# A hybrid encoder layer: half of two sets of transposes moved from the DMA queue to TensorE, a third buffer for the weights of down, and another order at the end of gate/up

## The chip, the cores and the metric

One NeuronCore of a Trainium2 chip runs the whole kernel. The metric is the device time of one execution in microseconds; the profile is one further execution, recorded instruction by instruction. Engines are TensorE (PE), VectorE (DVE), ScalarE (ACT), GpSimd (POOL) and SyncE (SP), which here issues all DMAs, in order.

## The reference

One layer over 2048 rows of width 1024, in f32:

```python
h = rmsnorm(r, norm1_g)
proj = h @ w_in                                   # q k v z beta alpha lx lg
dn_out  = rmsnorm(deltanet(fwd) + deltanet(bwd)) * silu(z)   # 4 heads, chunks of 64
lru_out = rmsnorm(gelu(lg) * (rglru(fwd) + rglru(bwd)))
r = r + concat([dn_out, lru_out]) @ w_out
h2 = rmsnorm(r, norm2_g)
gate = dwconv(h2 @ ffn_wg, ffn_conv_w) + ffn_conv_b
r = r + (gelu(gate) * (h2 @ ffn_wu)) @ ffn_wd     # width 2816
pg = sigmoid(rmsnorm(r, ple_norm_g) @ ple_wg + ple_bg)
return rmsnorm(r + pg * (p @ ple_wp), final_g)
```

## The kernel before, in words

Every large product is made from f16 halves: a number is split into a high part (ACT, a copy to f16) and the low rest (DVE, a subtraction), and three products hi x hi, lo x hi, hi x lo add up in PSUM. Gate/up and down use Strassen's scheme besides: seven products of half-size blocks, whose operands are sums of blocks that POOL adds before the split (`operands`, L1648; `split`, L1635). All of SBUF is one tile, `arena`, from which buffers are taken while the program is built.

**The order.** Each piece of work is a Python generator that yields `st(engine=price)` ahead of an instruction, `W(event)` to wait for another piece, `M(sizes)` for memory. `Sched.run` (L244) is a list planner: with the listed prices in ns it keeps a clock for each engine and always emits next the step that can start first, plus a small handicap for its priority (`LOOK` 20 ns for each step of priority). `ahead(ns)` is a DMA whose issuer does not wait. What it emits is the program; each engine and SP run their instructions in that order. A price thus changes no work, only the order. Prices that stand here: a DMA transpose 1300 (`norm`), 700 (`norm_pairs`, `ple`), 1000 (`out_lru`); the scan of the RG-LRU `c_tt(2048)`, some 2200 (L901).

**Start.** `norm1` (L653) loads x in blocks of four tiles of 128 rows; `norm` (L619) squares them (ACT, L632), forms the inverse root (`rsqrt`, eleven small DVE steps, L358 to L378), and for each tile splits the scaled row into h (ACT, L639) and l (DVE, L641) in one of three 4 KB buffers and transposes both by one DMA (L643) into `xT[b]`, the moving operand. `main` (L2485) runs the first three projections (q1, k1, lx1) quarter by quarter, one quarter for each block, and the small beta/alpha product (L787) with them; then the other projections follow. Weights go through `wprep` (L513): load, gain (POOL, L541), squares (ACT, L560), a sum over partitions (PE, L570), a power-of-two scale, split (L595, L597). `setup` (L459) forms constants on the side.

**Mixer.** Heads are prepared (`prep_head`), then run in a serial chain of 16 chunks, both directions together, one head after the other (`chain_head`, L1357); the RG-LRU streams run beside them.

**Output and normed rows.** `out_dn` (L1606), then `out_lru` (L1573) multiply the 16 tiles with w_out in the order `TILES`, and `out_add` (L1547) adds to the residual. As soon as two tiles are done, `norm_pairs` (L1717) squares them (L1736), forms the inverse root, scales them into `hb` (ACT, L1743), writes the residual out (L1747) and forms the seven right operands of Strassen's scheme from the four blocks of 128 x 512: sums on POOL, split (L1640, L1642) into one of four 2 KB buffers, and a DMA transpose (L1760) into `hU[u]`. There are eight pairs; `hU[0]` takes the first four, `hU[1]` the rest. Gate/up's unit (0, 0) needs `hU[0]`, unit (0, 1) `hU[1]`, and the first product of (0, 1) comes after four of (0, 0) (`units`, L1694).

**Gate/up, the seam, down.** `ffn` (L1998) runs 22 x 2 units (PE L1690), each evacuated by ACT (L1882) and DVE (L1887); convolution and gelu, POOL's multiplication (L1950), and a split of the result to DRAM (`act_post`, L1955). With the units of n = 20 done, `down_weights` (L2090) starts in two streams with one 8 KB raw buffer each: blocks 0, 2, 4, ... and 1, 3, 5, ... of w_d are loaded (L2100), combined on POOL (L1669) and split (L1644, L1646). Beside it run the products of p (`p_products`, L2332) and the first unit of down (`down_first`, L2202; PE L2233), which takes the blocks in order as they are ready. Then down runs seven more units, and the gated embedding follows (`ple`, L2397).

Of the kernel before, what the change touches and what calls it, by code (L numbers as in the profile page):

```python
# [16 lines left out]
S = SEQ = 2048  # L17
# [12 lines left out]
NI = 3  # L30

# [120 lines left out]
class Sched:  # L152
# [91 lines left out]
    def run(self):  # L244
        while self.streams:
# [37 lines left out]
LOOK = 20  # L283
PER = 2
# [56 lines left out]
class Kern:  # L341
# [117 lines left out]
    def setup(self):  # L459
# [32 lines left out]

        keep = self.keep
# [125 lines left out]
    def norm(self, rows, dst, done, hl, waits=()):  # L619
# [15 lines left out]
        def one(i):  # L635
            j, buf = yield from hl.take()
            h, l = buf.f16(D), buf.f16(D, at=2 * KB)
            yield st(act=c_act(D, 1))
            nc.scalar.activation(h, rows[i], AF.Copy, scale=y[:, i : i + 1])  # L639
            yield st(dve=c_stt(D))  # L640
            nc.vector.scalar_tensor_tensor(l, rows[i], y[:, i : i + 1], h, op0=ALU.mult, op1=ALU.subtract)  # L641
            yield st(dma=1300)
            nc.sync.dma_start_transpose(dst[i], buf.f16(2 * D))  # L643
            hl.done(j)
# [5 lines left out]
        for i in range(n):  # L650
            S.spawn(one(i), 3)

    def norm1(self, b, xb, hl):  # L653
# [17 lines left out]
        for o in range(0, 4, n):  # L671
            if b == 1 and o:
                yield W("xT", 0)
            ids = range(o, o + n)
            dst = [Tv[:, :, i * 128 : i * 128 + 128] for i in ids]
            S.spawn(self.norm([xb[4 * b + i].f32(D) for i in ids], dst, lambda i, o=o: done(o + i), hl, [W("x", 4 * b + i) for i in ids]), 1 if b else 0)
# [173 lines left out]
    def lru(self, ct):  # L850
# [26 lines left out]
        for d in range(2):  # L877
# [23 lines left out]
            yield st(dve=c_tt(SEQ))  # L901
# [455 lines left out]
    def chain_head(self, h):  # L1357
# [4 lines left out]
        if h:  # L1362
            yield W("chained", h - 1)
# [104 lines left out]
    def dn_out(self, h):  # L1468
# [9 lines left out]
        groups = ([6, 7, 8, 9], [4, 5, 10, 11], [2, 3, 12, 13]) + (([0, 1, 14, 15],) if h < 3 else ([1, 14], [0, 15]))  # L1478
# [94 lines left out]
    def out_lru(self):  # L1573
# [5 lines left out]
        def fetcher():  # L1579
            for j, t in enumerate(TILES):  # L1580
# [3 lines left out]
                yield ahead(1000)  # L1584
# [132 lines left out]
    def norm_pairs(self):  # L1717
# [8 lines left out]
        def begin(i):  # L1726
# [12 lines left out]
            if i == 7:  # L1739
                S.fire("last pair")  # L1740
            for k, t in enumerate(ts):
                yield st(act=c_act(D, 1))
                nc.scalar.activation(hb.f32(2, D)[:, k], self.rt(t), AF.Copy, scale=y[:, k : k + 1])  # L1743
# [10 lines left out]
            v = [hb.f32(2, D)[:, k, z * 512 : z * 512 + 512] for z in range(2) for k in range(2)]  # L1754
# [242 lines left out]

    def ffn(self):  # L1998
        S, A = self.S, self.A
        self.blk = yield M(8 * KB, 8 * KB)  # L2000
# [23 lines left out]
        def begin(n, u):  # L2024
            def f():
                if u == 0:
# [693 lines left out]
```

## Time and profile before

| | us |
|---|---|
| median of 3 runs (2795.54 to 2804.08) | 2795.77 |
| the profiled execution | 2800.17 |
| its span, first to last instruction | 2798.5 |
| PE busy (91%) | 2554.9 |
| DVE busy (65%) | 1827.6 |
| ACT busy (53%) | 1479.7 |
| POOL busy (33%) | 925.8 |

Mean granted clock of PE: 0.967 of full speed. In the lines of the profile, `L441` is the line of the kernel that made an instruction; a helper's line stands for all that call it. `arena<-arena` with a DMA is a transfer inside SBUF, here a transpose. `<-` in brackets names what ended the idle time before.

### The profile page before, as it was taken

How to read it: one execution, taken by the hardware profiler on the slowest of the kernel's cores; microseconds unless marked ns; L12 is line 12 of the kernel's file. 1: busy time of each engine (PE TensorE's matmuls, PEld its weight loads, DVE VectorE, ACT ScalarE, POOL GpSimd, SP SyncE). 2: the span in 40 equal slices, each digit the busy share in tenths (PEclk: the TensorE clock that was granted, in tenths of full speed). 3: DMA queues.
4: the chain of work that ended last, by engine and by line, in shares of the span. 5: the costliest groups of instructions: out<-in, count | busy, mean ns of one | idle time of the engine just before them, and what ended most of it. 6: DMA issues, size and time to landing. Idle time of an engine off the chain costs nothing.

```text
span 2798.5 us, 40157 instructions
## 1 busy us (share of the span) xinstructions
PE 2554.9 (91%) x13944; PEld 1291.9 (46%) x13944; DVE 1827.6 (65%) x3845; ACT 1479.7 (53%) x3094; POOL 925.8 (33%) x662
## 2 busy tenths in 40 slices
PE   5998899888989997995998999999997799999998
PEld 2554454466556664442443444444443244444443
DVE  6668877768785677486656777767768832222468
ACT  6576766764666675265655666666656410101323
POOL 1134434626320000033446566666655500000000
PEclk9999999999999998997999999999999999999999
DMA  9332242375455468488123333333326754457963
GB/s 243 80 91 80 60 133 61 88 224 167 107 160 166 124 205 290 121 194 189 58 81 100 98 104 103 102 104 104 103 64 200 232 174 144 165 166 236 278 170 139
DMA packets 479660, 399.21 MB, mean 143 GB/s; under 512 B 204897, under 2 KB 408673, under 8 KB 479457
## 3 DMA queue, kind: packets, MB, share of 16 engines
q1 hardware_dynamic: 479456, 396.64, 48.6%
q8 instruction: 110, 1.80, 0.3%
q14 instruction: 94, 0.76, 0.1%
HBM read 229.82 MB, written 128.97 MB: 128 GB/s over the span
## 4 chain that ended last, share of the span: by engine, by line
PE 50%; DVE 7%; ACT 3%; DMA 3%; issue 2%; POOL 2%; SPq 0%; ACTq 0%; DVEq 0%; POOLq 0%
PE P L1690 35%; PE P L441 12%; DVE arena L1646 2%; POOL arena L1669 1%; DMA arena<-arena 1%; PE P L2233 1%; ACT arena L1644 1%; DVE arena L1936 1%; DVE arena L1934 1%; DMA arena<-actd 1%; PE P L1427 1%; DVE arena L1642 0%; ACT arena L1640 0%; ACT arena L1736 0%; DMA arena<-in_w_gu_dram 0%
## 5 line engine op out<-in xcount | busy, mean ns | idle before, releaser
L1690 PE MATMUL P<-arena 128*128 128x512 f16 x5166 | 1132.9, 382 | 55.6 <-ACT arena L1882 30.9
L441 PE MATMUL P<-arena 128*128 128x512 f16 x4224 | 998.2, 386 | 34.9 <-DMA arena<-arena 11.9
L1690 PEld LDWEIGHTS <-arena 128*128 128x128 f16 x5166 | 508.3, 99 | 670.3 <-issue 55.3
L441 PEld LDWEIGHTS <-arena 128*128 128x128 f16 x4224 | 414.6, 100 | 483.8 <-issue 51.3
L1646 DVE SCALAR_TENSOR_TENSOR arena<-arena 128x512 f16<-128x512 f32 (+2 forms) x408 | 418.3, 1059 | 139.2 <-ACT arena L1644 138.8
L1644 ACT ACTIVATE arena<-arena 128x512 f16<-128x512 f32 (+2 forms) x408 | 281.2, 723 | 304.3 <-POOL arena L1669 144.8
L1669 POOL TENSOR_TENSOR arena<-arena 128x512 f32<-128x512 f32 (+1 forms) x200 | 343.2, 1722 | 276.0 <-DVE arena L1646 176.7
L2135 DVE SCALAR_TENSOR_TENSOR arena<-P,arena 128x512 f32<-128x512 f32 x95 | 70.0, 749 | 224.7 <-PE P L1690 189.7
L1806 POOL TENSOR_TENSOR arena<-arena 128x1024 f32<-128x1024 f32 x44 | 107.3, 2455 | 319.3 <-DMA arena<-in_w_gu_dram 310.1
L1950 POOL TENSOR_TENSOR arena<-arena 128x512 f32<-128x512 f32 x88 | 138.0, 1588 | 79.9 <-ACT arena L1940 47.9
L1882 ACT ACTIVATE arena<-P 128x512 f32<-128x512 f32 x176 | 102.5, 587 | 89.8 <-PE P L1690 73.1
L1225 POOL TENSOR_TENSOR arena<-arena 128x512 f32<-128x512 f32 x64 | 119.0, 1875 | 80.3 <-DVE arena L1175 62.7
L702 DVE SCALAR_TENSOR_TENSOR arena<-P,arena 128x511 f32<-128x511 f32 (+1 forms) x192 | 141.6, 741 | 2.0
L2186 ACT ACTIVATE arena<-arena 128x1024 bf16<-128x1024 f32 x16 | 16.9, 1056 | 236.0 <-DVE arena L2135 227.0
L1887 DVE TENSOR_TENSOR arena<-P,arena 128x512 f32<-128x512 f32 x132 | 90.0, 683 | 36.6 <-PE P L1690 35.7
L541 POOL TENSOR_TENSOR arena<-arena 128x1024 f32<-128x1024 f32 (+1 forms) x25 | 51.4, 2060 | 173.0 <-DMA arena<-in_w_in_dram 173.0
L1422 ACT ACTIVATE arena<-P,arena 128x128 f32<-128x128 f32 x128 | 46.8, 365 | 84.7 <-PE P L1416 59.9
L1433 DVE SCALAR_TENSOR_TENSOR arena<-arena,P 128x128 f32<-128x128 f32 x128 | 43.7, 342 | 52.7 <-PE P L1428 23.9
L1427 PE MATMUL P<-arena 128*128 128x128 f32 x256 | 60.4, 319 | 19.3 <-ACT arena L1425 12.7
L1547 DVE SCALAR_TENSOR_TENSOR arena<-P,arena 128x512 f32<-128x512 f32 x64 | 47.7, 746 | 43.2 <-PE P L441 43.2
L865 PE MATMUL P<-arena 128*128 128x512 f32 x128 | 64.8, 621 | 11.8 <-DVE arena L702 5.2
L1128 POOL TENSOR_TENSOR arena<-arena 128x512 f32<-128x512 f32 x32 | 39.2, 1226 | 109.4 <-DVE arena L1125 90.8
(233 smaller groups left out, 3384.8 us busy)
## 6 DMA issues: line engine op xcount, KB each, us to landing
arena<-hd SPq DMA_DIRECT2D x160, 256.0 KB, 3.2
actd<-arena SPq DMA_DIRECT2D x148, 256.0 KB, 2.4
arena<-actd SPq DMA_DIRECT2D x49, 640.0 KB, 4.0
arena<-in_w_gu_dram SPq DMA_DIRECT2D x44, 512.0 KB, 4.4
arena<-in_x_dram SPq DMA_DIRECT2D x32, 512.0 KB, 6.3
at<-arena SPq DMA_DIRECT2D x64, 256.0 KB, 2.8
arena<-at SPq DMA_DIRECT2D x128, 128.0 KB, 3.1
rd<-arena SPq DMA_DIRECT2D x32, 512.0 KB, 3.1
```

Source lines behind the costliest of these rows:

```text
L441: self.nc.tensor.matmul(out, l, r, start=(i + j == 0), stop=(i + j == m - 1))
L702: nc.vector.scalar_tensor_tensor(a[:, lo:hi], P[:, lo - sh : hi - sh], tp[:, j : j + 1], a[:, lo:hi], op0=ALU.mult, op1=ALU.add)
L1225: nc.gpsimd.tensor_tensor(pv[:, i % 2], a(slice(2 * i, 2 * i + 2)), b(slice(2 * i, 2 * i + 2)), op=ALU.mult)
L1427: nc.tensor.matmul(slot[0], k, tv[:, 2], start=True, stop=True)
L1644: nc.scalar.activation(hi, x, AF.Copy, scale=scale)
L1646: nc.vector.scalar_tensor_tensor(lo, x, scale, hi, op0=ALU.mult, op1=ALU.subtract)
L1669: nc.gpsimd.tensor_tensor(v[at], v[p], v[q], op=ALU.add if plus else ALU.subtract)
L1690: self.nc.tensor.matmul(out, l, r, start=(p in (1, 2, 5) and i + j == 0), stop=(p in (2, 3, 4) and i + j == m - 1), skip_group_check=True)
L1806: nc.gpsimd.tensor_tensor(v[i], v[i], c["g2"][:, :, None].to_broadcast([128, KT, 128]), op=ALU.mult)
L1882: nc.scalar.activation(d, P, AF.Copy)
L1887: nc.vector.tensor_tensor(d, P, d, op=ALU.add)
L1950: nc.gpsimd.tensor_tensor(v, v, U.buf.f32(2, 2, 4, 128)[:, i, s], op=ALU.mult)
```

## The change

**Start.** For blocks 0 and 1 of x (`TURN = 2`) `norm` scales the row in f32 (DVE), transposes it in eight pieces of 128 x 128 on PE into two PSUM banks (`turned`), copies the high part from PSUM (ACT) and subtracts (DVE, from PSUM), both straight into `xT`. Blocks 2 and 3 are left as they were. Priorities change (0 for turned tiles, 4 for the norms of blocks 1 to 3); the second half of block 1 no longer waits for block 0, and `setup`'s constants now do.

**Normed rows.** Pairs 1, 3, 5 and 7 transpose the four scaled blocks on PE, ACT copies them back over `hb`, and the seven operands are formed from the transposed blocks and split straight into `hU`. Pairs 0, 2, 4 and 6 are left.

**Prices.** DMA transposes: 2600 for 1300, 1400 for 700 and for 1000; the scan twice. From the units of n = 20 to the end of down's first unit (`more`) every nonzero price is raised, by 75 on ACT and by 250 on DVE and POOL.

**w_d.** Three streams with a raw buffer each: blocks (0, 3, 6, 8, 10), (1, 4, 7, 9), (2, 5).

`HEADS` is (0, 1, 2, 3), the order that stood there.

```diff
@@ Sched.run
             for e, c in cost.items():
                 if e in self.t:
+                    c += OVER[e] if c else 0
                     self.t[e] = t + c
+OVER = dict(pe=0, act=0, dve=0, pool=0, dma=0)
+SEAM = dict(act=75, dve=250, pool=250)
@@ setup
+        yield W("xT", 0)
         keep = self.keep
@@ norm
+    def turned(self, x, b):
+        P = self.bank(b)
+        for i in range(0, 512, 128):
+            self.nc.tensor.transpose(P[:, i : i + 128], x[:, i : i + 128], self.c["ident"])
+        return P
...
+            if turn:
+                yield W("ones")
+                v = buf.f32(D)
+                yield st(dve=c_tt(D) / 2)
+                nc.vector.tensor_scalar(v, rows[i], y[:, i : i + 1], None, op0=ALU.mult)
+                for k in (0, 4):
+                    b = yield st(pe=4 * 160, bank=1)
+                    P = self.turned(v[:, 128 * k : 128 * k + 512], b).rearrange("p (a n) -> p a n", n=128)
+                    yield st(act=c_act(512))
+                    nc.scalar.activation(dst[i][:, k : k + 4], P, AF.Copy)
+                    yield st(dve=c_tt(512))
+                    nc.vector.tensor_tensor(dst[i][:, 8 + k : 12 + k], P, dst[i][:, k : k + 4], op=ALU.subtract)
+                    S.release(b)
+                hl.done(j)
...
-            yield st(dma=1300)
+                yield st(dma=2600)
...
-            S.spawn(one(i), 3)
+            S.spawn(one(i), 0 if turn else 3)
@@ norm1
-            if b == 1 and o:
-                yield W("xT", 0)
...
-            S.spawn(self.norm(...), 1 if b else 0)
+            S.spawn(self.norm(..., b < TURN), 4 if b else 0)
@@ lru
-            yield st(dve=c_tt(SEQ))
+            yield st(dve=2 * c_tt(SEQ))
             nc.vector.tensor_tensor_scan(...)
@@ out_lru
-                yield ahead(1000)
+                yield ahead(1400)
@@ norm_pairs
+            if i % 2:
+                for x in v:
+                    b = yield st(pe=4 * 160, bank=1)
+                    P = self.turned(x, b)
+                    yield st(act=c_act(512))
+                    nc.scalar.activation(x, P, AF.Copy)
+                    S.release(b)
             def put(n, x):
+                if i % 2:
+                    to = self.hU[u][n].f16(8, 512)[:, :, o : o + 128]
+                    yield from self.split(x.rearrange("p (a n) -> p a n", n=128), to[:, 0:4], to[:, 4:8], 512)
+                    return
...
-                yield st(dma=700)
+                yield st(dma=1400)
@@ ffn
+    def more(self, n):
+        OVER.update(((e, n * c) for e, c in SEAM.items()))
     def ffn(self):
+        self.more(0)
...
+                if n == 20:
+                    self.more(1)
@@ down_weights
-        js = ((0, 2, 4, 6, 8, 10), (1, 3, 5, 7, 9))[par]
+        js = RAWS[par]
...
-            yield st(dma=2900, lag=0 if j == par else 3000)
+            yield st(dma=2900, lag=0 if j == js[0] else 3000)
@@ down
         yield from self.down_first(self.down_unit(0), bufs)
+        self.more(0)
@@ ple
-                    yield st(dma=700)
+                    yield st(dma=1400)
@@ main
-        for i in range(2):
+        for i in range(3):
             S.spawn(self.down_weights(i), 2)
```

More of the change, by code (lines that the diff above doesn't have):

```diff
@@ L30 @@
 NI = 3
+TURN = 2
+RAWS = ((0, 3, 6, 8, 10), (1, 4, 7, 9), (2, 5))
+HEADS = (0, 1, 2, 3)
 TILES = (7, 8, 6, 9, 5, 10, 4, 11, 3, 12, 2, 13, 1, 14, 0, 15)
@@ L616, in ring_stream, with norm @@
         self.S.fire("ring", par)
-    def norm(self, rows, dst, done, hl, waits=()):
+    def turned(self, x, b):
[3 more added lines that the diff above has]
+        return P
+    def norm(self, rows, dst, done, hl, waits=(), turn=False):
         nc, A, S = self.nc, self.A, self.S
@@ L636, in one @@
             j, buf = yield from hl.take()
[L637 to L641, printed above, removed]
-            yield st(dma=1300)
-            nc.sync.dma_start_transpose(dst[i], buf.f16(2 * D))
-            hl.done(j)
+            if turn:
[12 more added lines that the diff above has]
+                hl.done(j)
+            else:
+                h, l = buf.f16(D), buf.f16(D, at=2 * KB)
+                yield st(act=c_act(D, 1))
+                nc.scalar.activation(h, rows[i], AF.Copy, scale=y[:, i : i + 1])
+                yield st(dve=c_stt(D))
+                nc.vector.scalar_tensor_tensor(l, rows[i], y[:, i : i + 1], h, op0=ALU.mult, op1=ALU.subtract)
+                yield st(dma=2600)
+                nc.sync.dma_start_transpose(dst[i], buf.f16(2 * D))
+                hl.done(j)
             left[0] -= 1
@@ L671, in norm1 @@
         for o in range(0, 4, n):
-            if b == 1 and o:
-                yield W("xT", 0)
             ids = range(o, o + n)
             dst = [Tv[:, :, i * 128 : i * 128 + 128] for i in ids]
-            S.spawn(self.norm([xb[4 * b + i].f32(D) for i in ids], dst, lambda i, o=o: done(o + i), hl, [W("x", 4 * b + i) for i in ids]), 1 if b else 0)
+            S.spawn(self.norm([xb[4 * b + i].f32(D) for i in ids], dst, lambda i, o=o: done(o + i), hl, [W("x", 4 * b + i) for i in ids], b < TURN), 4 if b else 0)
             for i in ids:
@@ L1740, in begin @@
                 S.fire("last pair")
+            hv = hb.f32(2, D)
             for k, t in enumerate(ts):
                 yield st(act=c_act(D, 1))
-                nc.scalar.activation(hb.f32(2, D)[:, k], self.rt(t), AF.Copy, scale=y[:, k : k + 1])
+                nc.scalar.activation(hv[:, k], self.rt(t), AF.Copy, scale=y[:, k : k + 1])
             smb.free()
@@ L1753, in begin @@
             yield W("hT", u)
-            v = [hb.f32(2, D)[:, k, z * 512 : z * 512 + 512] for z in range(2) for k in range(2)]
+            v = [hv[:, k, z * 512 : z * 512 + 512] for z in range(2) for k in range(2)]
+            if i % 2:
[5 more added lines that the diff above has]
+                    S.release(b)
             def put(n, x):
+                if i % 2:
+                    to = self.hU[u][n].f16(8, 512)[:, :, o : o + 128]
+                    yield from self.split(x.rearrange("p (a n) -> p a n", n=128), to[:, 0:4], to[:, 4:8], 512)
+                    return
                 j, buf = yield from ring.take()
                 yield from self.split(x, buf.f16(512), buf.f16(512, at=KB), 512)
-                yield st(dma=700)
+                yield st(dma=1400)
                 nc.sync.dma_start_transpose(self.hU[u][n].f16(8, 512)[:, :, o : o + 128], buf.f16(1024))
@@ L2528, in main @@
                     end(G, then)
-        for h in range(4):
+        for h in HEADS:
             S.spawn(self.prep_head(h), PR["prep"])
```

11 lines of the change are left out of this document (6 added, 5 removed).

## The prediction

> **What bounds the kernel now.** The page's first line gives the span; the profiled execution took 2800.2 us, 1.7 us of it outside the span. It lies 4.4 us above the median of the three runs (2795.8), so I sum against 2800.2 and take the sum off 2795.8.
>
> ```profile
> span 2798.5 us, 40157 instructions
> ```
>
> Then the table of stretches, cut where TensorE (PE) changes its work. Columns: stretch, length, busy time and instructions of PE, weight loads, DVE, ACT, POOL; then clock, DMA share, GB/s.
>
> ```profile
> 0.00:31.00 31.00, 1.76 (x6) 1.50 (x6) 19.99 (x74) 18.42 (x28) 5.57 (x12) 1.00 0.80 210
> 31.00:56.00 25.00, 20.64 (x174) 10.36 (x175) 17.03 (x62) 18.32 (x28) 5.69 (x3) 0.97 1.07 284
> 56.00:100.00 44.00, 44.00 (x365) 22.48 (x364) 27.28 (x62) 15.62 (x22) 0.00 (x0) 0.94 0.65 138
> 100.00:210.00 110.00, 105.72 (x573) 57.59 (x572) 75.22 (x182) 83.57 (x152) 37.04 (x33) 1.00 0.29 84
> 210.00:840.00 630.00, 554.94 (x4048) 323.82 (x4046) 495.76 (x1142) 403.34 (x1070) 279.09 (x277) 0.95 0.42 120
> 840.00:1081.00 241.00, 218.72 (x1433) 150.90 (x1432) 160.98 (x595) 172.64 (x495) 11.19 (x5) 0.96 0.59 186
> ...
> 1171.00:1258.00 87.00, 86.41 (x389) 38.79 (x390) 65.59 (x146) 48.83 (x82) 28.84 (x21) 0.96 0.85 184
> 1258.00:1302.00 44.00, 12.63 (x47) 4.86 (x44) 31.44 (x70) 26.46 (x45) 19.04 (x15) 0.67 1.03 235
> ...
> 1400.00:1540.00 140.00, 123.72 (x553) 55.44 (x552) 85.26 (x109) 76.06 (x126) 76.78 (x43) 0.94 0.29 89
> ...
> 2100.00:2241.00 141.00, 102.88 (x435) 43.49 (x432) 118.10 (x130) 76.53 (x116) 77.54 (x48) 0.92 0.69 217
> 2241.00:2612.00 371.00, 369.95 (x1707) 167.34 (x1708) 101.25 (x197) 43.47 (x66) 0.00 (x0) 1.00 0.57 182
> ```
>
> PE is the bound nearly everywhere, and the places where it is not are few: the first 31 us (29 idle) and up to 56 (4 more), the mixer from 210 to 1081 (97 idle, in many small pieces), 1258 to 1302 (31 idle), 1400 to 1540 (16) and the seam between gate/up and down, 2100 to 2241 (38). The change touches three of them: the start, the end of the normed rows, and the seam. Who holds PE at the first two is in the waits and in the order of time. First the start:
>
> ```profile
> 7.04 0.17 DVE L358 TENSOR_SCALAR arena<-arena 128x2 f32<-128x2 f32 x1 [7.04 <-ACT arena L632]
> ...
> 15.84 0.17 DVE L403 TENSOR_SCALAR arena<-arena 128x8 f32<-128x8 f32 x1
> ...
> 19.09 10.36 SPq L643 DMA_TRANSPOSE arena<-arena  x3
> ...
> 31.17 7.07 PE L441 MATMUL P<-arena 128*128 128x512 f16 x26 [7.74 <-DMA arena<-arena]
> ```
>
> ```profile
> 55.17 2.74 PE L441 MATMUL P<-arena 128*128 128x512 f16 x6 [4.19 <-DMA arena<-arena]
> ...
> 57.99 10.76 PE L441 MATMUL P<-arena 128*128 128x512 f16 x42
> ```
>
> Both starts of PE wait for a transpose by DMA (arena<-arena): the first projection for block 0 of x, the second quarter for block 1. Three issues alone keep SyncE's queue 10.4 us. Then the normed rows, from the waits of PE, the line of the transposes, and the DMA view from 1171 to 1302:
>
> ```profile
> PE P L1690 <- DMA arena<-arena: 16.1, 1, 16.1
> PE P L1690 <- ACT arena L1882: 15.7, 1, 15.7
> ```
>
> ```profile
> L1760 SPq DMA_TRANSPOSE arena<-arena x56: 1231/1293/2295, 1201.9 to 1313.1; - x56
> ...
> DMA to landing us min/median/max: 3.0/3.4/5.1
> ```
>
> ```profile
> q1 hardware_dynamic: 70834, 26.21, 91.2%
> ...
> arena<-arena SPq DMA_TRANSPOSE x50, 3.3
> ```
>
> 56 transposes by 1.29 us of issue are 72 us of one queue within 111 us, and the 16 DMA engines are 91% taken in those 131 us though only 26 MB move. The DMA path, not an engine, is what the pairs queue for here; ACT and DVE have room (49 and 66 of 87 us).
>
> **Start.** Removed for blocks 0 and 1: 8 transposes by DMA, 8 ACT copies and 8 DVE subtractions over 1024. Added for each tile: one DVE scale over 1024 in f32, eight PE transposes, two ACT copies out of PSUM, two DVE subtractions that read PSUM. Prices from rows that do the same elsewhere:
>
> ```profile
> 153.71 0.60 PE L1036 MATMUL P<-arena 128*128 128x128 f32 x4
> 154.15 3.62 PE L441 MATMUL P<-arena 128*128 128x512 f16 x16
> ```
>
> ```profile
> L1887 DVE TENSOR_TENSOR arena<-P,arena 128x512 f32<-128x512 f32 x132 | 90.0, 683 | 36.6 <-PE P L1690 35.7
> ...
> L902 DVE TENSOR_TENSOR_SCAN arena<-arena 128x2048 f32<-128x2048 f32 x8 | 37.9, 4739 | 0.0
> ...
> L641 DVE SCALAR_TENSOR_TENSOR arena<-arena 128x1024 f16<-128x1024 f32 x16 | 21.9, 1387 | 3.6 <-ACT arena L639 3.4
> ```
>
> ```profile
> L1882 ACT ACTIVATE arena<-P 128x512 f32<-128x512 f32 x176 | 102.5, 587 | 89.8 <-PE P L1690 73.1
> ```
>
> Four transposes take 0.44 us of PE's stream (154.15 less 153.71). The scale has no row of its kind; I bound it by twice a 512 DVE pass from PSUM (1.4) and half of that (0.7, if f32 from SBUF runs at double rate), and take 1.0, as it reads one operand where L641 reads two. Then DVE pays 1.0 + 2 x 0.68 = 2.4 a tile where it paid 1.39: +1.0, over four tiles +4. ACT is level (2 x 0.59 for one copy of 1024). When can PE start? DVE had 20.0 us of work in the first 31, from 7.04 on. About 13 steps of setup like the one at 15.84 (2.2 us) now wait for block 0, and some 3.3 us of it belonged to block 1 (a chain of small steps and one L641). So 20.0 - 5.5 + 4 = 18.5, densely packed from 7.04: 25.5. The weights of the first projections are prepared on the same engines and are in this count. PE starts about 5.5 us earlier; with the scale at its ends 4 to 7.
>
> Block 1 then has 20 us of PE work as cover, and loads that no longer stand behind transposes in SyncE's queue. The wait of 4.2 us goes, and so does the half clock after it: 6 matmuls in 2.74 and 42 in 10.76, where 48 at the 3.62/16 of the row above are 10.9, is 2.6 us lost. Against it stand 8 groups of transposes in PE's stream, 3.5 us. Net 3.3. **Start: 9 us**, bounds 3 to 14. Blocks 2 and 3 stay with DMA, and are needed some 9 us sooner; eight transposes fewer ahead of them in the queue (3.4 us each by the three above) cover that. PE is full from 56 to 210 (149.7 of 154), so the gain reaches 210.
>
> **Mixer.** The order of all engines is computed from listed prices, and two change: the scan doubles (about 4.4 us, close to the measured 4.74) and transposes by DMA double. No work is added, but every in-order queue may be dealt out anew. Nothing in the trace prices this; 97 us of PE idle are there to be gained or added to. I take 0, with -15 to +15.
>
> **Normed rows.** For pairs 1, 3, 5 and 7: 28 transposes go, from SyncE's queue 28 x 1.29 = 36 us and from the DMA engines as much or more; four blocks each go PE, ACT and back in place (4 x 0.44 PE, 4 x 0.59 ACT), and the sums on POOL and the 7 splits write straight into the operand, without the ring of four. The splits themselves stay. What ends last then? PE's own stretch of output products, which ended at 1258, gets 12 groups of transposes ahead of its end, +5.3. The last pair is odd; after PE's last tile it needs an addition, two squares, the chain of small steps, two scalings, four rounds through PE and ACT, and one split:
>
> ```profile
> L1640 ACT ACTIVATE arena<-arena 128x512 f16<-128x512 f32 x52 | 31.1, 621 | 30.3 <-DMA arena<-arena 23.6 <-DVE arena L373 3.9 <-DVE arena L369 1.6
> L1743 ACT ACTIVATE arena<-arena 128x1024 f32<-128x1024 f32 x16 | 17.8, 1138 | 12.0 <-DVE arena L378 10.8 <-DVE arena L1642 1.3
> L1736 ACT ACTIVATE arena<-arena 128x1024 bf16<-128x1024 f32 x16 | 16.7, 1043 | 0.1
> ```
>
> ```profile
> L1642 DVE TENSOR_TENSOR arena<-arena 128x512 f16<-128x512 f32 x52 | 40.2, 780 | 19.0 <-ACT arena L1640 18.4
> L1547 DVE SCALAR_TENSOR_TENSOR arena<-P,arena 128x512 f32<-128x512 f32 x32 | 23.7, 742 | 14.5 <-PE P L441 14.5
> ```
>
> 0.7 + 2.4 + 3.5 (eleven small steps, 1.9 us at the 0.17 of the row at 7.04, more beside POOL: an estimate) + 2.3 + 4 x 1.5 (0.44 + 0.59 and two handovers) + 1.4 = 16. Is there a backlog before it? ACT needs per even pair 2.4 + 2.3 + 7 x 0.62 = 9.0 and per odd pair 2.4 more; DVE 7 x 0.78 + 4 x 0.74 and the small steps, 11 to 12; PE 10.9 (87 us for eight) + 0.9. They are close, so I allow 4. PE resumes at 1258 + 5.3 + 16 + 4 = 1283 where it resumed at 1302.4:
>
> ```profile
> 1302.42 19.25 PE L1690 MATMUL P<-arena 128*128 128x512 f16 x78 [16.11 <-DMA arena<-arena]
> ```
>
> **Normed rows: 19 us**, bounds 5 (backlog 18) to 24 (none, small steps at 2). Behind PE's transposes, which wait for ACT's scaling, stand the output products of the next tile: a late pair stops PE. ACT's copies stand ahead of the next squares; their cover is PE's queue.
>
> [...]
>
> **Seam.** A third buffer for raw w_d lets block 2 load with 0 and 1; the prices of ACT, DVE and POOL are raised for ordering only. The view by groups from 2100 to 2245, and who waited for these loads:
>
> ```profile
> L1646 DVE SCALAR_TENSOR_TENSOR arena<-arena 128x512 f16<-128x512 f32 x82 | 93.5, 1194 | 12.6 <-ACT arena L1644 12.6
> L2349 DVE TENSOR_SCALAR arena<-P,arena 128x512 f32<-128x512 f32 x16 | 11.6, 738 | 6.1 <-DMA ppd<-arena 6.1
> ```
>
> ```profile
>   ACT arena L1644: 20.2, 4
> ...
> DMA to landing us min/median/max: 4.9/6.5/9.9
> ```
>
> ACT waits 20.2 us in four places for raw rows; DVE, 118 of 141 us busy, loses 12.6 of its 23 idle us to that. More than 17 (the idle without the 6.1 behind ppd) can't be had unless DVE has less to do. One block of lead hides some of four waits: **7 us**, bounds -5 (8 KB fewer for other buffers, other order) to 17. PE has 38 us idle there, so it follows.
>
> Sum: 9 + 0 + 19 + 7 = 35: 2800.2 becomes 2765, and off the median 2761. After 2241 PE is full until 2612, so nothing gives it back; of the last stage's transposes only the price changes.
>
> **The rivals.** Hidden transfers: the pairs are late for ACT's and DVE's sake (two in-order engines with small steps stretched beside POOL), and DMA is busy only because it is given the time. The wait for ACT (15.7) speaks for it, 91% and the wait for DMA (16.1) against. The normed rows then give 0, the sum is 16: 2780. [...]
>
> The gain of the start is lost: the mixer ends with the serial chain of four heads, and a new order costs it 10 more. 35 - 9 - 10 = 16, again 2780. For it: DVE is busy 496 of 630 us there. Against: nothing is added to it.
>
> It does nothing that shows: the seam at -5, rows at 5, start at 3 less a mixer that takes that back: 2788 to 2804.
>
> More: the weights of gate/up are loaded while SyncE's queue is free, so that the 16 idle us from 1400 to 1540 shrink by 12 too: 2749; with a mixer gain, 2735.
>
> Slower: PE stops at the odd pairs. Its queue is in order; if ACT is late as before (the last pair took 44 us where its own steps take 16: 28 late), PE stands in the middle of its output products for that once, and 1.5 us for each of 12 rounds (18), and runs 26 us of them at the clock of 0.67 seen from 1258 on (+13). It resumes at 1258 + 5 + 28 + 18 + 13 + 16 = 1338, 36 late instead of 19 early: 35 - 55 = -20, 2816. It decides from 16 us later than before (1318), where it has eaten start and seam.
>
> **How the numbers follow.** Chances: forecast 0.50, its own range 2743 to 2778; hidden transfers 0.12; start lost 0.11; more 0.10; nothing 0.08; slower 0.09. Predicted 2761. The range runs from 2736 to 2794: it leaves out the slower case, most of "nothing" above 2794 and the far end of "more". A change of 0.3%, 8.4 us, is about what a measurement of this kernel can tell from none. Faster by more: 0.82; within: 0.09; slower: 0.09.
>
> **What would show it.** Right: the first long run of projections begins at 24 to 27 us and has no wait for DMA at its second quarter; transposes by DMA on the line of the pairs are 28, their queue share from the first pair to the last falls well below 91%; PE resumes gate/up about 25 us after its last output product, not 44; fewer waits for w_d in the seam. Wrong: PE idle inside the output products (slower), the gap of 44 us unchanged in length with DMA idle (hidden transfers), or a mixer whose length from 210 to 1081 changes by more than 15 us.

## The result, and the profile after

The kernel became slower. After: 2830.13 us median of 4 runs (2827.14 to 2833.24); before, on the same chip: 2795.65 us of 4 runs (2789.31 to 2804.08). The ratio is 1.0123, 95% interval 1.0107 to 1.0139, some 34 us. The forecast was 2761, and 2830 lies outside its range and beyond its slower rival (2816).

First some stretches of the kernel after, with the columns of the prediction's table; 1640 to 2100 is added. The second fence has the row of before for that stretch.

```profile
span 2825.6 us, 40377 instructions
```

```profile
0.00:31.00 31.00, 11.88 (x47) 8.04 (x48) 21.67 (x72) 19.84 (x35) 7.93 (x13) 0.91 0.66 260
31.00:56.00 25.00, 24.19 (x212) 14.20 (x211) 24.45 (x82) 20.59 (x35) 3.79 (x2) 0.98 0.52 162
56.00:100.00 44.00, 44.00 (x409) 23.14 (x407) 27.99 (x70) 13.72 (x20) 0.00 (x0) 1.00 0.44 89
...
210.00:840.00 630.00, 559.24 (x4119) 323.80 (x4117) 493.77 (x1145) 409.70 (x1083) 281.15 (x276) 0.96 0.42 119
...
1640.00:2100.00 460.00, 438.96 (x2010) 199.07 (x2008) 314.56 (x405) 278.63 (x489) 257.53 (x140) 0.98 0.29 89
2100.00:2241.00 141.00, 109.87 (x459) 46.74 (x457) 114.85 (x136) 77.98 (x116) 71.53 (x43) 0.90 0.68 218
2241.00:2612.00 371.00, 367.82 (x1707) 166.73 (x1705) 116.85 (x208) 51.82 (x79) 13.12 (x8) 1.00 0.54 176
```

```profile
1640.00:2100.00 460.00, 460.00 (x2149) 210.52 (x2148) 324.50 (x428) 295.41 (x520) 279.33 (x145) 1.00 0.32 97
```

The start did what it was to do: 47 instructions of PE in the first 31 us where there were 6. But look at 1640 to 2100, a stretch that the prediction's table leaves out: PE was full there, and no instruction of it was changed. PE did 2149 matmuls in it before and does 2010 now: 139 at 0.214 us (460 / 2149) are 30 us. For 21 of them PE is idle (460.00 less 438.96), the rest goes with a lower granted clock (0.98 for 1.00). The view of PE's waits over the whole span has these rows:

```profile
PE P L1723 <- ACT arena L1927: 35.3, 9, 6.2
PE P L452 <- DVE arena L2499: 17.2, 1, 17.2
PE P L635 <- DVE arena L660: 15.4, 3, 11.6
...
PE P L635 <- ACT arena L1777: 10.6, 3, 6.8
PE P L1723 <- ACT arena L1673: 10.0, 1, 10.0
```

L1723 is the product of gate/up (L1690 before), L1927 the evacuation of its bank by ACT (L1882 before). This wait is not new (30.9 us in three places before), but before none of it lay between 1640 and 2100, where PE never stopped. The wait for L2499 is new. L635 are the transposes of `turned`. The order of time shows the first stop once in each cycle of gate/up (one gate and one up block, 336 matmuls):

```profile
1816.12 24.72 PE L1723 MATMUL P<-arena 128*128 128x512 f16 x106 [3.42 <-ACT arena L1927]
...
1894.20 23.04 PE L1723 MATMUL P<-arena 128*128 128x512 f16 x106 [3.44 <-ACT arena L1927]
...
1970.59 24.73 PE L1723 MATMUL P<-arena 128*128 128x512 f16 x106 [3.43 <-ACT arena L1927]
```

A cycle takes 78.1 and 76.4 us (1816.12 to 1894.20 to 1970.59). Before it took 72.8, from these rows:

```profile
1677.72 32.54 PE L1690 MATMUL P<-arena 128*128 128x512 f16 x150
...
1750.52 32.53 PE L1690 MATMUL P<-arena 128*128 128x512 f16 x150
```

So a cycle loses 5.3 or 3.6 us: the stop of 3.4, and in the longer one 1.7 by a lower clock after it (last section). Who is late? One stop, as ACT, POOL and DVE saw it:

```profile
1803.30 4.08 ACT L1977 ACTIVATE arena<-arena 128x2048 f32<-128x2048 f32 x2 [1.13 <-DVE arena L1974]
1807.29 1.32 ACT L1677 ACTIVATE arena<-arena 128x512 f16<-128x512 f32 x2
1810.00 0.72 ACT L1677 ACTIVATE arena<-arena 128x512 f16<-128x512 f32 x1 [1.40 <-POOL arena L1702]
1813.27 0.72 ACT L1677 ACTIVATE arena<-arena 128x512 f16<-128x512 f32 x1 [2.55 <-POOL arena L1702]
...
1814.30 0.58 ACT L1927 ACTIVATE arena<-P 128x512 f32<-128x512 f32 x1
1815.48 1.09 ACT L1927 ACTIVATE arena<-P 128x512 f32<-128x512 f32 x2 [0.60 <-DVE arena L1981]
```

```profile
1804.07 9.17 POOL L1702 TENSOR_TENSOR arena<-arena 128x512 f32<-128x512 f32 x4 [9.59 <-DVE arena L1679]
```

```profile
1805.58 6.54 DVE L1979 SCALAR_TENSOR_TENSOR arena<-arena 128x2047 f32<-128x2047 f32 x2
1812.04 5.60 DVE L1981 SCALAR_TENSOR_TENSOR arena<-arena 128x2047 f32<-128x2047 f32 x2
```

The evacuation stands in ACT's queue behind splits (L1677) that wait for POOL's sums (L1702). The four sums began late, and the last two of them meet the convolution passes on DVE (L1979, L1981). The second evacuation waits for the third of these passes besides. The order in the queues agrees: from 1680 to 2040 us DVE, POOL and ACT each repeat one order exactly, cycle after cycle, in either kernel, but it is another order. On DVE, with c for a convolution pass and e for an addition out of a bank, it was c e c e c e c and is c c c c e; POOL's first sum, which stood among the multiplications of gelu and up, now stands behind all of them.

The new wait is in the last stage, at 2703, where PE stops for 17.2 us. Behind it is a load of p's product that came late. In SyncE's queue the first four (L2489) follow the last transposes of `ple` (L2463), and DVE waits 19.3 us for one of them; before, the first went out at 2576.

```profile
2687.84 4.00 SPq L2463 DMA_TRANSPOSE arena<-h3d  x2
2692.98 1.85 SPq L2489 DMA_DIRECT2D arena<-ppd  x4
```

```profile
2698.41 0.69 DVE L2505 TENSOR_TENSOR arena<-arena 128x512 f32<-128x512 f32 x1 [19.27 <-DMA arena<-ppd]
```

Where the 27 us of the span lie (2798.5 to 2825.6), from four instants of each profile:

| us | before | after | change |
|---|---|---|---|
| to the first addition of an output product | 1086.0 | 1087.9 | +1.9 |
| from there to the last evacuation of gate/up | 1041.7 | 1056.7 | +15.0 |
| to the last product of down's first unit | 128.6 | 122.5 | -6.1 |
| to the end | 542.2 | 558.5 | +16.3 |

### The profile page after: what moved, and what is told of

Same layout as the page of the kernel before. It is cut to its first block, busy times and chain, and to the rows that moved or that the text cites. A ratio compares the mean times of both kernels' runs of the same rounds, so it can differ in the third digit from the quotient of the medians.

```text
span 2825.6 us, 40377 instructions
## 1 busy us (share of the span) xinstructions
PE 2585.0 (91%) x14072; PEld 1317.0 (47%) x14072; DVE 1865.3 (66%) x3861; ACT 1491.2 (53%) x3120; POOL 933.5 (33%) x662
## 5 line engine op out<-in xcount | busy, mean ns | idle before, releaser
L1723 PE MATMUL P<-arena 128*128 128x512 f16 x5166 | 1138.9, 383 | 48.8 <-ACT arena L1927 35.3
L452 PE MATMUL P<-arena 128*128 128x512 f16 x4224 | 992.6, 385 | 46.8 <-DVE arena L2499 17.2
L1723 PEld LDWEIGHTS <-arena 128*128 128x128 f16 x5166 | 509.5, 99 | 665.5 <-issue 73.4
L1679 DVE SCALAR_TENSOR_TENSOR arena<-arena 128x512 f16<-128x512 f32 (+2 forms) x408 | 436.3, 1106 | 88.3 <-ACT arena L1677 87.4
L1702 POOL TENSOR_TENSOR arena<-arena 128x512 f32<-128x512 f32 (+1 forms) x200 | 372.7, 1868 | 357.1 <-DVE arena L1679 253.7
L1677 ACT ACTIVATE arena<-arena 128x512 f16<-128x512 f32 (+2 forms) x408 | 281.1, 723 | 273.2 <-POOL arena L1702 129.9
L1995 POOL TENSOR_TENSOR arena<-arena 128x512 f32<-128x512 f32 x88 | 130.5, 1502 | 129.3 <-ACT arena L1985 91.2
L1927 ACT ACTIVATE arena<-P 128x512 f32<-128x512 f32 x176 | 102.5, 589 | 103.2 <-PE P L1723 95.9
L1932 DVE TENSOR_TENSOR arena<-P,arena 128x512 f32<-128x512 f32 x132 | 90.4, 686 | 98.7 <-PE P L1723 94.5
L1851 POOL TENSOR_TENSOR arena<-arena 128x1024 f32<-128x1024 f32 x44 | 90.3, 2057 | 189.7 <-DMA arena<-in_w_gu_dram 189.7
L1257 POOL TENSOR_TENSOR arena<-arena 128x512 f32<-128x512 f32 x64 | 123.7, 1950 | 64.0 <-DVE arena L1207 55.7
L1309 PE MATMUL P<-arena 32*32 32x32 f32 (+1 forms) x1792 | 64.1, 210 | 20.3 <-POOL arena L1257 5.2
L2110 ACT ACTIVATE arena<-arena 128x256 bf16<-128x256 f32 x88 | 35.9, 408 | 74.3 <-DMA arena<-in_w_d_dram 74.0
```

The lines of the kernel that those rows point to most:

```text
L452: self.nc.tensor.matmul(out, l, r, start=(i + j == 0), stop=(i + j == m - 1))
L1257: nc.gpsimd.tensor_tensor(pv[:, i % 2], a(slice(2 * i, 2 * i + 2)), b(slice(2 * i, 2 * i + 2)), op=ALU.mult)
L1677: nc.scalar.activation(hi, x, AF.Copy, scale=scale)
L1679: nc.vector.scalar_tensor_tensor(lo, x, scale, hi, op0=ALU.mult, op1=ALU.subtract)
L1702: nc.gpsimd.tensor_tensor(v[at], v[p], v[q], op=ALU.add if plus else ALU.subtract)
L1723: self.nc.tensor.matmul(out, l, r, start=(p in (1, 2, 5) and i + j == 0), stop=(p in (2, 3, 4) and i + j == m - 1), skip_group_check=True)
```

## The experiments

The theory at this point: the loss is in the order alone. The listed prices decide into which of two cycles gate/up falls and where the loads of p's products stand. The rival: the work that was added slows gate/up itself, and the order is only seen beside it. Ratios are to the kernel before, timed beside each kernel (medians of 2795.65 to 2799.23 us). One profiled execution has a spread too: in eleven profiles, of after and of ten kernels below with the same order up to there, the first addition of an output product lies between 1084.0 and 1092.5 us. A difference of a few us at that instant, between two single profiles, is therefore not safe.

**One price back in the kernel after.**

```diff
@@ norm_pairs
-                yield st(dma=1400)
+                yield st(dma=700)
                 nc.sync.dma_start_transpose(self.hU[u][n]...)
```

> The kernel after, with one number back: the listed price of the normed rows' DMA transposes is 700 again instead of 1400. No instruction is added or removed. Theory (the order is the cause: the doubled price made the planner settle gate/up into a cycle in which four convolution passes stand together on VectorE beside POOL's sums): the cycle of before comes back, a cycle of gate/up takes 72 to 73 us again instead of 78, and the loads of p's products are again ahead of the last transposes, so that PE's stop of 17 us in the last stage goes: 2783 to 2803 us. Rival (the new transposes on PE and the direct writes into the operands slow gate/up themselves, the order is only seen beside it): cycles stay near 78 us, 2815 to 2835 us.

2795.72 us; ratio to before 0.9997 (0.9988 to 1.0005). The order of gate/up is that of before again, from 1640 to 2100 PE is full:

```profile
1640.00:2100.00 460.00, 460.00 (x2151) 210.63 (x2150) 322.29 (x425) 291.26 (x513) 271.75 (x142) 1.00 0.33 102
```

All 34 us are gone with one number, and the transposes on PE are still there. Against before, the section from the first output product to the end of gate/up is 1031.7 us, 10 shorter (6 in two later runs without the raised prices). The odd pairs are in that, but so are other prices; beside the scan's price alone they earn 4 (below).

**The same number in the kernel before.** The converse, with none of the change's work: 1200 for 700.

```diff
@@ norm_pairs (kernel before)
-                yield st(dma=700)
+                yield st(dma=1200)
```

> The kernel before, with one number changed: the listed price of the normed rows' DMA transposes is 1200 instead of 700. None of the change's work is in it. Theory (the planner settles gate/up into one of two cycles, and the price only decides into which): by its written order this kernel has the same cycle as the kernel after, so gate/up's cycles take 78 us instead of 72.7 and the time is 2812 to 2828 us. Rival (the cycle is slow only together with the new transposes on PE or the other memory layout): within 4 us of before.

2831.28 us, ratio 1.0113 (1.0095 to 1.0131): the kernel before loses as much as the whole change did, and a little more than the theory gave. Its stretch and its waits from 1642 to 2022 are those of after:

```profile
1640.00:2100.00 460.00, 438.79 (x2017) 198.82 (x2015) 322.17 (x407) 283.81 (x500) 263.14 (x142) 0.99 0.29 89
```

```profile
PE P L1690 <- ACT arena L1882: 17.1, 5, 3.4
```

**A price between.** 1200 for 1400 in the kernel after.

> The kernel after with the pairs' price at 1200 instead of 1400. By its written order it has the cycle of before, while prices of 1100, 1300 and 1400 give the slow one. Theory (only the selected cycle matters, not the price's size): PE is full from 1640 to 2100 us, 2792 to 2806 us. Rival (a higher price of these transposes costs more, step by step): between the runs at 700 and 1400, some 2820 us.

2792.00 us, ratio 0.9981 (0.9968 to 0.9994). PE is full from 1640 to 2100. No effect of the price's size shows: 700 and 1200 give one cycle in this kernel, 1400 the other. The rival falls with these three runs.

**The price of the last stage back**, alone, and with the pairs' price.

```diff
@@ ple
-                    yield st(dma=1400)
+                    yield st(dma=700)
```

> The kernel after, with only the listed price of the last stage's DMA transposes back at 700 instead of 1400. Theory (this price set the loads of p's products behind the transposes in SyncE's queue): PE's stop of 17 us in the last stage goes, gate/up stays at 78 us a cycle: 2814 us (2808 to 2820). Rival (the loads are late because gate/up and down are late or for want of memory, whatever that price): 2826 to 2834 us with the stop still there.

> The kernel after, with both of these prices back at 700. Theory: if the pairs' price alone restores both orders, the same as with it alone within 5 us; if the last stage needs its own price, 12 to 17 us less: 2778 to 2795 us either way, below the kernel before, as start, seam and normed rows then keep what they gained (0, 7 and 3.5 us). Rival (the added work itself is the loss): 2814 to 2835 us.

Alone: 2816.48 us (1.0071, 1.0058 to 1.0084), 14 less than after; the first four loads of p's products go out at 2628 and the stop of PE is gone. Both: 2799.16 us (1.0012, 1.0004 to 1.0021), no better than the pairs' price alone, as that by itself had moved these loads ahead to 2608.

**The third raw buffer alone**, in the kernel before.

```diff
@@ down_weights
-        js = ((0, 2, 4, 6, 8, 10), (1, 3, 5, 7, 9))[par]
+        js = ((0, 3, 6, 8, 10), (1, 4, 7, 9), (2, 5))[par]
...
-            yield st(dma=2900, lag=0 if j == par else 3000)
+            yield st(dma=2900, lag=0 if j == js[0] else 3000)
@@ main
-        for i in range(2):
+        for i in range(3):
             S.spawn(self.down_weights(i), 2)
```

> The kernel before with the third raw buffer and the three streams for w_d alone, none of the raised prices. Theory (the lead of one block gives the seam its 7 us): down's first product begins about 7 us earlier and the time is 2789 us (2785 to 2792). Rival (the raised prices for the end of gate/up made the gain, by another order of the splits): 2793 to 2798 us.

2804.66 us, ratio 1.0036 (1.0025 to 1.0048): 9 to 10 us slower, so both guesses fail. The seam takes 133.1 us instead of 128.6 and the end 547.6 instead of 542.2. The waits in the seam say why the cover was no gain:

```profile
ACT arena L1644 <- DMA arena<-in_w_d_dram: 9.0, 3, 5.5
```

```profile
DVE arena L2135 <- PE P L2233: 28.4, 1, 28.4
DVE arena L1646 <- ACT arena L1644: 8.7, 7, 6.1
```

ACT's wait for raw rows fell from 20.2 to 9.0 us, just as foreseen, and DVE's wait behind it from 12.6 to 8.7. But DVE then waits 28.4 us in one place for down's first products, 10.3 before: the splits were not what ended last. Down's first unit begins on PE at 2196.25 here and at 2189.76 before, and PE runs its last 33.6 us without a stop.

**The turned start alone**, in the kernel before (`turned`, the new `norm`, its priorities and waits; prices as before).

> The kernel before with the turned start alone (blocks 0 and 1 of x on PE, the new priorities and waits; old prices). Theory (the first projections begin 4 us earlier, but the serial chain of heads does not, so the output products begin when they did): 2793 to 2798 us. Rival, as predicted (the gain reaches the end): 2784 to 2790 us.

2790.00 us, ratio 0.9962 (0.9947 to 0.9977). It is faster than both kernels, with the lowest ratio of all that compute the whole layer. The first projections begin at 27.80 us (31.17 before), the first addition of an output product at 1077.9, 8.0 early. So the theory that the chain of heads eats the gain fell; something else in the change takes it.

**The scan's price alone**, in the kernel before.

```diff
@@ lru
-            yield st(dve=c_tt(SEQ))
+            yield st(dve=2 * c_tt(SEQ))
             nc.vector.tensor_tensor_scan(...)
```

> The kernel before with the listed price of the RG-LRU's scan doubled, nothing else. Theory (this price re-deals the mixer and costs it what the start wins there: the output products began at 1094 us in the run that held it with the old start, 1084 before and 1076 with the turned start and the old price): the output products begin 8 to 12 us later and the time is 2804 to 2812 us. Rival (the late mixer of that run came from the odd pairs or from the spread between executions): 2793 to 2800 us.

2811.88 us, ratio 1.0060 (1.0047 to 1.0073). The time came as the theory had it, the place only in part. The first addition of an output product is at 1090.5 us, 4.5 late in this profile. The section to the end of gate/up is 4.4 us longer and the last stage 5.6, the seam 3.0 shorter: PE's wait for the pairs' transposes is 25.5 us in this profile and was 16.1.

**The odd pairs without the start**, in the kernel before, with the scan's price doubled (without that, the planner finds no room for the buffers; the odd pairs alone at the old prices could not be tried).

> The kernel before with the odd pairs of normed rows transposed on PE alone, and the listed price of the scan doubled (with the old one the planner finds no room for the buffers); the cycle of gate/up is that of before. Theory (the pairs give back about 12 us between the first output product and the end of gate/up, 3.5 at once and the rest in the first cycles): 2781 to 2788 us. Rival, as predicted (19 us at the gap alone): 2772 to 2779 us. Second rival (nothing): 2793 to 2798 us.

2810.72 us, ratio 1.0040 (1.0025 to 1.0054). The first addition is at 1094.2, 8.2 late; the order up to there is that of the scan's price alone, so the difference to its 1090.5 is spread. The section to the end of gate/up is 1041.9, level with before and 4.2 shorter than with the scan's price alone. All three expectations missed, as none had charged the scan's price. Set against the run before it, the pairs are no loss. What they do to PE is in its order of time: the wait for DMA is gone, and PE stands at its own transposes until ACT has scaled the rows.

```profile
1248.43 1.12 PE L1760 MATMUL P<-arena 128*128 128x128 f32 x4 [6.23 <-ACT arena L1743]
1305.45 1.09 PE L1760 MATMUL P<-arena 128*128 128x128 f32 x4 [16.45 <-ACT arena L1743]
```

**The seam undone in the kernel after** with the pairs' price back (two streams, no raised prices), and the same with the price of `ple` back too.

> The kernel after with the pairs' price back at 700 and the seam undone (two streams with two raw buffers, no raised prices). It holds the turned start and the odd pairs on PE. Theory (the third buffer costs 9 us, start 0, pairs win 12): 2783 to 2790 us, faster than both kernels. Rival (the third buffer and the raised prices win together): 2796 to 2803 us.

> The kernel after with the pairs' price back, the seam undone, and the last stage's price back too. The run with all that but the last took 2812.1 us and still had the 17.6 us stop of PE in the last stage. Theory (that stop is the loads of p's products behind the doubled transposes): the stop goes, 2794 to 2800 us. Rival (another wait takes its place): 2808 to 2814 us.

2812.10 us (1.0040, 1.0027 to 1.0052) and 2797.22 us (1.0002, 0.9993 to 1.0010): the first missed both its expectations, the second came as its theory had it. The seam is shorter, 127.8 us against 133.9 with the three streams, yet the first of these kernels had the 17.6 us stop in the last stage again, with the first loads of p's products at 2679. With the price of `ple` back they go out at 2618, and by the ratios 11 us come back. So that price costs 11 to 14 us in two contexts and nothing in another (the first run above has it as well).

**Start and odd pairs together** at old prices, the scan at 1.05 of its price, and the same with PE's transposes put further back:

```diff
@@ norm_pairs
-                    b = yield st(pe=4 * 160, bank=1)
+                    b = yield st(pe=4 * 160, bank=1, lag=4000)
```

> Turned start and odd pairs on PE, all listed prices as before but the scan's at 1.05 of the old one (at 1.00 the planner finds no room for the buffers), two raw buffers, no raised prices, the cycle of before in gate/up. Theory (the start keeps its 10 us once the mixer isn't re-dealt, the odd pairs win 2 to 8 more): 2781 to 2789 us. Rival (the pairs cost as in the run that had them without the start, or 1.05 re-deals the mixer as 2 does): 2796 to 2806 us.

> The same, with the PE transposes of the odd pairs listed as ready 4 us later, so that the planner puts them further back in PE's queue; the cycle of gate/up is the same. Theory (PE stops at them for ACT's scaling, in order, 20 to 24 us where they stand now): the stop shrinks below 10 us and the time is 4 to 12 us under the run without the delay. Rival (PE only waits there for what it would wait for later, the last pair's operands): the wait moves to the product behind it and the time is within 3 us.

2819.98 us (1.0079, 1.0067 to 1.0092) and 2813.55 us (1.0060, 1.0048 to 1.0073). The first run missed both its expectations. Its first addition of an output product is at 1101.3 us, and at 1106.7 in the second run. The kernel that took 2797.22 us has the same work and differs in three prices alone (the scan's twice, `norm`'s transposes 2600, `out_lru`'s 1400): there it is at 1090.2. So with this work the old prices give the slower mixer; which of the three does it, no run separates. The delay of the transposes gives 6 us: PE's wait at them falls from 24.2 to 10.9 us, but 14.9 us of waiting for DVE appear at a sum of the weights. Most of the wait moves on, as the rival had it, and a part is gained.

**What holds PE in the slow cycle.** Four versions of the kernel after, in the slow cycle, each with some work left out: the convolution's third tap; the low parts of every second set of weights; POOL's sums for the weights; sums and tap.

The edits for the sums and for the tap, the first shortened:

```diff
@@ operands (key ("pw", n), n > 3)
-                nc.gpsimd.tensor_tensor(v[at], v[p], v[q], ...)
+                nc.gpsimd.tensor_tensor(v[at][:, :, 0:16], v[p][:, :, 0:16], v[q][:, :, 0:16], ...)
@@ gate_tile
-        nc.vector.scalar_tensor_tensor(a[:, :-1], g[:, 1:], tp[:, 2:3], a[:, :-1], ...)
+        pass
```

> The kernel after without the third tap of the convolution (one pass of 2.84 us over 2047 on VectorE left out for each tile, two for each cycle, 5.7 us); the order is otherwise that of after, the slow cycle. Theory (the block of convolution passes beside POOL's sums holds up the sums, the splits behind them and so ACT's evacuation that PE waits for): PE's stop of 3.4 us a cycle goes below 1 us, cycles take 73 to 75 us, the time is 2798 to 2812 us. Rival (the stop comes from the order of splits on ACT alone, whatever VectorE does): the stop stays near 3.4 us, 2824 to 2832 us.

> The kernel after with the low parts of every second set of gate/up weights formed over 128 x 64 instead of 128 x 512 (seven passes of 1.1 us a cycle, about 6 us of VectorE's time left out, outside the convolution block); the order is that of after, the slow cycle. Theory (the place of the convolution block costs, not VectorE's load): the stop stays at 2.5 us or more a cycle, 2820 to 2832 us. Rival (VectorE's load is the cause): the stop goes as with the tap left out, 2798 to 2812 us.

> The kernel after with POOL's sums for gate/up's weights formed over 128 x 64 instead of 128 x 512 (work left out, from the fifth set on); the order is that of after, the slow cycle. Theory (two chains end at the same evacuation, ACT's queue behind POOL's sums and the convolution's last pass; either alone holds PE): the stop stays at 2.6 to 3.4 us a cycle, its wait now behind the convolution; 2815 to 2830 us. Rival (the splits behind POOL's sums are the whole cause): the stop goes below 1 us, 2796 to 2808 us.

> The same and without the convolution's third tap, so that both chains are shorter. Theory (the two together hold PE): the stop goes below 1 us a cycle, PE is busy for over 455 of the 460 us from 1640 to 2100, 2794 to 2806 us. Rival (neither: ACT's own work ahead of the evacuation, two convolution steps of 2 us and four splits, is enough to stop PE): the stop stays at 2 us or more, 2812 to 2820 us.

| left out | PE's stop in a cycle, us | PE busy, 1640 to 2100 | median, us | ratio |
|---|---|---|---|---|
| nothing (after) | 3.4 | 438.96 | 2830.13 | 1.0123 |
| third tap | 2.7 | 442.98 | 2817.74 | 1.0078 |
| low parts, outside the block | 3.4 | 439.46 | 2827.47 | 1.0113 |
| sums | 1.2 | 446.75 | 2799.02 | 1.0004 |
| sums and tap | 1.2 | 450.29 | 2798.45 | 0.9999 |

VectorE's load as such is not the cause, and the theory of two chains that each hold PE fell: the sums alone bring the stop to a third. The profile of that run shows ACT's four splits in one piece, and the convolution passes shorter as well:

```profile
1787.70 1.51 POOL L1702 TENSOR_TENSOR arena<-arena 128x64 f32<-128x64 f32 x4 [11.71 <-DVE arena L1679]
```

```profile
1789.21 4.61 DVE L1979 SCALAR_TENSOR_TENSOR arena<-arena 128x2047 f32<-128x2047 f32 x2
1793.73 4.61 DVE L1981 SCALAR_TENSOR_TENSOR arena<-arena 128x2047 f32<-128x2047 f32 x2
```

```profile
1790.92 2.55 ACT L1677 ACTIVATE arena<-arena 128x512 f16<-128x512 f32 x4
...
1796.37 1.57 ACT L1927 ACTIVATE arena<-P 128x512 f32<-128x512 f32 x3 [2.50 <-PE P L1723]
```

The cause in the slow cycle is thus the place of POOL's sums: so late, and beside the convolution passes, that the splits behind them hold up ACT, and with ACT the evacuation that PE needs.

The third tap did not test whether the passes delay the sums. With it left out the first two passes stand where they stood, and the last two sums still take 3.20 and 3.19 us, where the two ahead of them take 1.28 each (the rows are from two narrow windows):

```profile
1798.87 3.20 POOL L1702 TENSOR_TENSOR arena<-arena 128x512 f32<-128x512 f32 x1
1802.14 3.19 POOL L1702 TENSOR_TENSOR arena<-arena 128x512 f32<-128x512 f32 x1
```

So the passes cost these sums 2 x 1.9 = 3.8 us, more than the 1.5 us of stop that go with the sums (2.7 less 1.2). That the stop would go if the sums stood elsewhere beside the same work is an estimate from these rows; no run moved the sums alone. The 0.7 us that go with the tap are the second evacuation's wait (0.60 above). The 1.2 us that stay are two evacuations in a row: in the last fence ACT is idle until PE's last product ends, and PE goes on after the second of the three. How much of the 34 us between the first row and the fourth comes from the cycle alone is open: the sums are shorter at the end of gate/up and in its first cycles too.

## Why the prediction was wrong

**What bounds the kernel** was read rightly, with one omission: a stretch where PE is full was taken as one that can't change. PE was full from 1640 to 2100 because the in-order queues happened to be dealt out in a cycle that fits, and the change re-deals them.

**The start** (9 us, PE at 25.5): right in mechanism and in sum. PE's first long run begins at 27.24 us, 3.9 earlier in place of 5.5; the wait for DMA at the second quarter is gone. The scale, put at 1.0 us between 0.7 and 1.4, took 0.75 (median of eight, 0.74 to 2.46; L660, 1024 f32 from SBUF), where the subtraction over 512 from PSUM took 0.68 (L667): 1.8 times the elements in a ns. Alone the edit wins 0.38%, 10.6 us (6 to 15).

**The mixer** (0, from -15 to +15): the first addition of an output product is 1.9 us late, with a start that alone makes it 8.0 early. The new order of the mixer takes about 10. The scan's price is part of that: it makes this instant 4.5 and 8.2 late in the two runs that hold it with the old start. What the other prices do to it is not separated. That is the rival "the gain of the start is lost", in mechanism and nearly in price; it came true, and it was not the main loss.

**The normed rows** (19 us): the step that failed is "I allow 4" for the backlog, which measured 20. PE resumes gate/up at 1298.94, not 1283. It waits 8.1 us for ACT's scaling inside the output products, which end at 1270.65 and not at 1263, and then needs 28.3 us where the prediction had 20. The queue did empty: there are 28 transposes, and PE waits no more for one. The DMA view from 1171 to 1302:

```profile
q1 hardware_dynamic: 48983, 20.90, 69.8%
```

Its share was 91.2%. What came last next was ACT, not DMA: PE stands 10.6 us for L1777 (the scaling), 10.0 for L1673 (a split). This is the slower rival's mechanism at a third of its price (20 us where it had 28 + 18 + 13), in place of the two waits of before, 32 us together; it stays short of that rival's point of decision.

**The seam** (7 us): after shows 6.1 less, but for another reason. Gate/up ends 17 us late there, and the seam's work on POOL, DVE and ACT had gone on meanwhile. With the right cycle the three streams make it 133.9 us, 5.3 longer. The failing step is "PE has 38 us idle there, so it follows": the transfer was hidden, and PE did not follow.

**Gate/up and the last stage**: the main loss. The step that failed is that the sum has no term for them, so it puts what the new order does there at nothing. The prediction wrote "Nothing in the trace prices this" of the mixer alone, "nothing gives it back" of what follows, and of the last stage "only the price changes". A price is an edit here, and it acts on all that is planned behind it. It cost the section with gate/up 25 us (1056.7 against 1031.7 with the one price back) and the last stage 16. No rival had this mechanism. It could have been one, worked out from the rows there: in 460 us with PE at 460.00, any stop of one engine's queue can only lose.

## What to carry to other kernels

Where a planner or a hand-written list sets the order of in-order queues, a changed price or priority is a change to every stage behind it, and the stages where the bounding engine is at 100% have only something to lose: give the re-deal a term and a rival of its own, for each such stage. Before an edit is judged, look whether the repeating stages still have the order that they had; if not, time the edit again with that order, or the order alone without the edit. Of this change, the turned start at old prices (0.9962) was worth keeping, and it was found only by taking the parts one by one.

## What the runs showed of the hardware

**Passes and sums ended in turn.** These are passes and sums of the stop at 1816 us in the kernel after, in order of time, each row from a narrow window of its own because the view joins neighbours:

```profile
1805.42 1.28 POOL L1702 TENSOR_TENSOR arena<-arena 128x512 f32<-128x512 f32 x1
1805.58 3.26 DVE L1979 SCALAR_TENSOR_TENSOR arena<-arena 128x2047 f32<-128x2047 f32 x1
1806.77 3.20 POOL L1702 TENSOR_TENSOR arena<-arena 128x512 f32<-128x512 f32 x1
1808.76 3.35 DVE L1979 SCALAR_TENSOR_TENSOR arena<-arena 128x2047 f32<-128x2047 f32 x1
1810.05 3.19 POOL L1702 TENSOR_TENSOR arena<-arena 128x512 f32<-128x512 f32 x1
1812.04 3.35 DVE L1981 SCALAR_TENSOR_TENSOR arena<-arena 128x2047 f32<-128x2047 f32 x1
1815.30 2.34 DVE L1981 SCALAR_TENSOR_TENSOR arena<-arena 128x2047 f32<-128x2047 f32 x1
```

With no pass beside it a sum took 1.27 us (the first of the four, at 1804.07), and with POOL idle a pass took 2.34 (the last row). The rows between seem to last longer, but from the end of one row to the end of the next it is 2.1 us for a pass and 1.1 for a sum, in turn: 1806.70, 1808.84, 1809.97, 1812.11, 1813.24, 1815.39. So these rows read as if each instruction, begun while the other engine's still ran, stood until that one was done and then ran at its own speed: by their ends, no pass and sum here made headway together. The four sums took 9.17 us with two of them at 1.27 and 1.28, and not because all four were slow. An addition on DVE that reads one operand from PSUM was not held up: L1932 took 0.69 us at 1804.97, beside the first sums, and 0.68 at 1817.57, with POOL idle. A small step on DVE was: in the kernel before, L365 took 1.25 us at 1216.34, just after POOL began two sums (L1669, 2.62 us from 1216.31), and 0.16 at 1232.28, with POOL idle.

**A short stop of PE cost more than itself.** After the stop at 1816.12 of the kernel after, 106 matmuls took 24.72 us, after that at 1894.20 the same 106 took 23.04: 1.7 us between two stops of 3.42 and 3.44 us. The granted clock just after either stop (the number behind POOL's) differs, and with it the matmuls done, 12 and 18:

```profile
1816.10:1820.00 3.90, 3.88 (x12) 1.49 (x12) 3.90 (x4) 3.90 (x3) 1.56 (x1) 0.65 0.00 0
1894.20:1898.00 3.80, 3.80 (x18) 1.76 (x18) 3.80 (x4) 3.80 (x3) 1.48 (x1) 1.00 0.01 2
```

Of six stops of 3.42 to 3.44 us in this profile, four were followed by a lower clock (0.55 to 0.65) and two by 1.00, so length alone did not decide. With the third tap left out the stops are 2.7 us long: after those at 1807.51 and 1883.16 the same 106 matmuls took 23.04 us, after that at 1958.82 91 took 21.49, 1.7 more than at that pace. With the sums left out 72 matmuls after a stop of 1.17 us took 15.70, which is that pace; the clock of that kernel from 1640 to 2100 is 1.00. What else decides, no run here shows.
